# Weight conversions one step behind their raw loads, in program order on ScalarE, and handed out among more products, in a two-layer decoder step

## The chip, the cores and the metric

The kernel runs on one core of a Trainium2 chip. The metric is device time in microseconds (us) of one execution; the number given for a kernel is the median of several runs. The engines are TensorE (PE, matrix products), VectorE (DVE), ScalarE (ACT), GpSimd (POOL) and SyncE (SP), which here only issues transfers (DMAs). Each engine works through its own instructions strictly in the order in which they stand in its program; an instruction that waits holds up all behind it.

## The reference

One inference step of a two-layer decoder, for a prompt of 2048 positions and 8 sample streams of 4 positions. Layer 0 is a gated recurrent mixer (four heads), layer 1 is sliding-window attention over keys and values that are computed once. The change is in layer 0:

```python
def gla_mixer(h, state0, norm_g, w_in, w_gate2, b_gate, out_norm_g, w_out):
    u = rmsnorm(h, norm_g)
    proj = u @ w_in
    q, k, v, gate, g_low = jnp.split(proj, ...)
    log_a = jax.nn.log_sigmoid((g_low @ w_gate2 + b_gate)) / A_GATE_NORMALIZER
    o, state = gla_recurrence(heads(q) * dk ** -0.5, heads(k), heads(v), heads(log_a), state0)
    o = rmsnorm(o, out_norm_g).reshape(bsz, seq_len, BRANCH_WIDTH)
    return (o * jax.nn.silu(gate)) @ w_out, state
...
def step(state, blk):
    b = jnp.cumsum(ac, axis=2)
    scores = einsum('bhtd,bhsd,bhtsd->bhts', qc, kc, exp(b_t - b_s) where s <= t)
    out = einsum('bhtd,bhdv->bhtv', qc * exp(b), state) + einsum('bhts,bhsv->bhtv', scores, vc)
    new_state = exp(b_last) * state + einsum('bhsd,bhsv->bhdv', kc * exp(b_last - b), vc)
```

The model width is 1024, a head has 128 key and 512 value columns, and all inputs, weights and outputs are float32.

## The kernel before

**Products.** A float32 product is made of three fp16 matmuls: each operand is split into a high part (the fp16 rounding) and a low part (the rest), and high x high, high x low and low x high are added up in one PSUM bank. A weight therefore passes three steps before TensorE can use it: a DMA of 256 KB from DRAM into a float32 tile `wraw` (L224; three buffers), the high part on ScalarE (L192: scale by the norm's gain and round), and the low part on VectorE (L193: scaled weight less the high part). Both parts go into a tile `W` of a pool of `NW` buffers. `Unit.load` does all three for one half of a unit, and `Unit.steps` gives the two halves as two steps. `Cols` is a column group of a weight, made of units: a head's v weights and its g (gate) weights are four units each, eight steps; its q and k weights (`qk`) are units of 256-wide pieces.

**Order.** The program is written as lists of small steps that `run`, `weave` and `mix` play in turn; `weave(a, b)` spreads b among the steps of a. A scheduler then makes the order of each engine from the traced steps, by a model of time and by priorities. `tc.keep_in_program_order(x)` ties an instruction behind the one traced before it on its engine. It was used only for the weights that are converted ahead for layer 1 (`prepare`, tile `pst`, written back to DRAM as `pre`); these are done one step behind their raw load, by the list `pending` and `flush`.

**Layer 0.** It runs from about 100 to about 1130 us of the span, over four heads h and four blocks j of 512 positions, in the loop over n = 4h + j (block 14 is n = 14). Block n's own products are, for each of four groups c of 128 positions, v (`vg_steps(c, (0,))`) and gate (`vg_steps(c, (1,))`), 24 matmuls each (`pj`). Between them stand the q and k products of the next block (`qk_steps`, evicted by ACT at L457 into KQ), the decays of the next block (`decay_steps`: L379 to L385 with two table loads on ACT, E and bt), the recurrence of the block's chunks (`chunk_steps`: v is evicted at L192 and L193; `kv`, `o` and `lev` are its matmuls; S is the state, Sh and sth its fp16 halves, X and qe the decayed keys and queries), and the gate's eviction `sg` (L500) and the gated result `og` (L617). `og` is split into `ogT`, transposed by a DMA (L630, `ogk`), and written to DRAM (L631, `ogd`); that write stands on SP behind its transposition and waits for its end.

At the end of a head (j = 3, "last") the weights of the next head come in: all eight v steps run in one piece after the v products, ahead of the last three gate products, and all eight g steps in one piece behind the last gate product. The q and k weights come in one block earlier, at c = 0 of j = 2. The block behind that, j = 0 of the next head ("late"), makes its gate product for c = 0 after the next block's q and k products. In the last head the out-projection's weights come instead: `wo` and `wo1` are its two halves, with tiles in `uT` buffers and `W` buffers; 4 steps of `wo` and 8 of `wo1` run in block 14, `wo.steps()[4:]` (12 steps) in place of the next head's v, `wo1.steps()[8:]` in place of g.

Of the kernel before, what the change touches and what calls it, by code (L numbers as in the profile page):

```python
# [10 lines left out]
F16 = mybir.dt.float16  # L11
# [8 lines left out]
P = 128  # L20
# [5 lines left out]
AH, DK, DV = 4, 128, 512  # L26
# [24 lines left out]
NW = 12  # L51
# [24 lines left out]
def _body(tc, nc, cp, sb, ps, dr, i, o):  # L76
# [6 lines left out]
    def T(tag, shape, dt, bufs=None):  # L83
        return sb.tile(shape, dt, tag=tag, name=nm(tag), **({} if bufs is None else {"bufs": bufs}))
# [61 lines left out]
    def weave(main, fill):  # L146

        main, fill = list(main), list(fill)
        done = 0
        for n, f in enumerate(main):  # L150
            f()
            upto = len(fill) * (n + 1) // len(main)
            for g in fill[done:upto]:
                g()
            done = upto
        for g in fill[done:]:
            g()

    def run(steps):
        for f in steps:  # L160
            f()

    def mix(a, b):

        out = []
        weave([lambda f=f: out.append(f) for f in a], [lambda f=f: out.append(f) for f in b])
        return out

    def behind(steps, n):


        def one(f):
            with tc.high_priority(offset=-n):
                f()

        return [lambda f=f: one(f) for f in steps]
# [15 lines left out]
            put(act(hi, src, AF.Copy, scale=sc))  # L192
            dve.scalar_tensor_tensor(lo, src, sc, hi, ALU.mult, ALU.subtract)  # L193

    pending = []

    def flush():
        while pending:
            pending.pop(0)()

    class Unit:

# [5 lines left out]
        def steps(self):  # L208
            if self.pre is not None:
                return [self.fetch]  # L210
            return [lambda half=half: self.load(half) for half in range(2)]

        def raw(self, half):

# [25 lines left out]
                split((dst(0)[:, d], dst(1)[:, d]), raw[:, d], gs[:, k : k + 1], put=put)  # L240

        def load(self, half):
            if self.t is None:
                self.t = T("W", [P, 2, 1024], F16, NW)
            self.convert(half, self.raw(half), lambda hl: self.t[:, hl, half * 512 : half * 512 + 512])

        def prepare(self):

            uniq[0] += 1
            self.pre = dr.tile([P, 2, 1024], F16, tag=f"pre{uniq[0]}", name=f"pre{uniq[0]}")  # L250

            def one(half):
                raw = self.raw(half)
                flush()

                def rest():
                    t = T("pst", [P, 2, 512], F16, 2)
                    self.convert(half, raw, lambda hl: t[:, hl], tc.keep_in_program_order)
                    nc.gpsimd.dma_start(self.pre[:, :, half * 512 : half * 512 + 512], t)  # L259

                pending.append(rest)

            return behind([lambda half=half: one(half) for half in range(2)], 200)
# [10 lines left out]
    class Cols:  # L274
# [7 lines left out]
                self.units.append(Unit([(0, ncol, w[k0 * P : (k0 + self.per) * P, c0 : c0 + ncol])], ncol, gs, [(k0 + n) % ng for n in range(self.per)]))  # L282

        def steps(self):
            return [f for u in self.units for f in u.steps()]

        def prepare(self):
            return [f for u in self.units for f in u.prepare()]
# [564 lines left out]
    gw = [GroupW(g) for g in range(NKV)]  # L853
# [3 lines left out]
    def form_steps(m):  # L857

        b, f = {}, {}

        def load():
            two = T("KQ", [P, 2, 512], F32, 1)
            for n, (r, z) in enumerate(((0, 0), (0, 1), (1, 0), (1, 1))):
                t = T("wraw", [P, 512], F32, 3) if n < 2 else two[:, n - 2]
                k = UP[m] + 2 * r
                nc.sync.dma_start(t, i["b_w_out"][0][k * P : (k + 1) * P, z * 512 : z * 512 + 512])
                b[r, z] = t
            f[0], f[3], f[5] = b[0, 0], b[1, 0], b[1, 1]

        def put(n):  # L870
            def sub(x, y):
                t = T("sth", [P, 512], F32, 2)
                pool.tensor_tensor(t, x, y, ALU.subtract)
                f[n] = t

            if n == 2:
                sub(b[0, 1], b[0, 0])
            elif n == 1:
                sub(b[1, 1], f[2])
            elif n == 4:  # L880
                sub(b[1, 1], b[0, 1])
            elif n == 6:
                sub(b[1, 0], f[1])
            t = T(tags[0], [P, 2, 512], F16, 2)
            tags.append(tags.pop(0))
            split((t[:, 0], t[:, 1]), f[n], SWB)
            nc.gpsimd.dma_start(wfd[n][:, m], t)

        return behind([load] + [lambda n=n: put(n) for n in (0, 2, 1, 3, 6, 5, 4)], 200)

    prep = [f for w in gw for f in w.prepare()] + behind([flush], 200) + [f for m in range(8) for f in form_steps(m)]

    def some(n=2):
        out = prep[:n]
# [17 lines left out]
    prep = [lambda n=n, w=w, hf=hf: rope_table(n, w, hf) for n in range(2) for w in range(2) for hf in range(2)] + prep  # L912

    hw = {0: head_weights(0)}
    cur = Blk(0, 0, hw[0])
# [14 lines left out]
    f = T("pst", [P, 7, 64], F32, 2)  # L930
# [4 lines left out]
    wo, wo1 = (out_w(i["a_w_out"][0], half, gs_o) for half in range(2))  # L935
    box_o = {}

    def wo_aside():
# [3 lines left out]
        for u in range(4):  # L942
            wo1.units[u].t = t[:, u]

    blocks = [(h, j) for h in range(AH) for j in range(NBL)]
    weave([f for c in range(4) for f in cur.vg_steps(c, (0,))] + cur.vg_steps(0, (1,)), cur.level_steps() + cur.decay_steps())
    prev_tail = []
    samp = None
    sparts = []

    for n, (h, j) in enumerate(blocks):
        nxt = None
# [9 lines left out]
        last = j == NBL - 1  # L962
        late = j == 0 and h > 0
        if n > 0:
            weave(cur.vg_steps(0, (0,) if late else (0, 1)), prev_tail)
        if last:
            samp = SampleA(h, cur.w)
            for f in samp.proj_steps():
# [6 lines left out]
        if last:  # L975
            ch = [cur.chunk_steps(c) for c in range(3)]
            weave([f for c in range(1, 4) for f in cur.vg_steps(c, (0,))], ch[0] + lv[:3] + ch[1][:3] + lv[3:5] + ch[2][:3])
            run(hw[h + 1].v.steps() if h + 1 < AH else wo.steps()[4:])
            for c in range(1, 4):
                weave(cur.vg_steps(c, (1,)), (ch[c - 1][3:] if c > 1 else []) + lv[3 + c * 2 : 5 + c * 2])  # L980
            for f in ch[2][3:]:
                f()
            run(hw[h + 1].g.steps() if h + 1 < AH else wo1.steps()[8:])
        else:
            for c in range(3):
                if n == len(blocks) - 2:
                    if c == 0:
                        wo_aside()
                    more = (wo1.steps()[:8] + wo.steps()[:4])[c * 4 : c * 4 + 4]
                else:  # L990
                    more = side[c * 2 : c * 2 + 2] if n < 2 else some(PR[j])
                weave(cur.vg_steps(c + 1, (0, 1) if n else (1,)), mix(cur.chunk_steps(c) + lv[(0,3,6)[c]:(3,6,8)[c]], sparts[(0,3,7)[c]:(3,7,99)[c]]) + more)
                if j == NBL - 2 and h + 1 < AH and c == 0:
                    hw[h + 1] = head_weights(h + 1)
                    for u in hw[h + 1].qk:
                        for f in u.steps():
                            f()
            sparts = []
        if n == 0:
            gain(gs_o, i["a_out_norm"][0], later)  # L1000
# [55 lines left out]
        cur = nxt  # L1056
# [794 lines left out]
```

## Time and profile before

| what | value |
|---|---|
| median of 3 runs | 2803.41 us |
| the 3 runs | 2795.48, 2803.41, 2803.76 us |
| the profiled execution, its own time | 2805.45 us |
| its span | 2803.6 us |
| mean granted clock of TensorE | 0.989 |
| first 100 us of the span and some more | start-up, layer 0's first projections |
| about 100 to 1130 us | layer 0, 16 blocks |
| from about 1130 us | the out-projection, shared keys and values, layer 1 |

The page's engines: PE is the matrix product's engine, PEld its weight loads (beside PE), and DVE, ACT, POOL, SP as above. The DMA queue of SP is shown as SPq. A row of the timeline gives the start, the duration, the engine, the line, the operation, output<-input by the program's names, and in brackets the idle time of that engine just before it and what released it. Because each engine works in order, an ACT instruction that waits for a DMA also keeps the ones behind it; the release named in another engine's row is then that ACT instruction and not the DMA.

### The profile page before, as it was taken

How to read it: one execution, taken by the hardware profiler on the slowest of the kernel's cores; microseconds unless marked ns; L12 is line 12 of the kernel's file. 1: busy time of each engine (PE TensorE's matmuls, PEld its weight loads, DVE VectorE, ACT ScalarE, POOL GpSimd, SP SyncE). 2: the span in 40 equal slices, each digit the busy share in tenths (PEclk: the TensorE clock that was granted, in tenths of full speed). 3: DMA queues.
4: the chain of work that ended last, by engine and by line, in shares of the span. 5: the costliest groups of instructions: out<-in, count | busy, mean ns of one | idle time of the engine just before them, and what ended most of it. 6: DMA issues, size and time to landing. Idle time of an engine off the chain costs nothing.

```text
span 2803.6 us, 51849 instructions
## 1 busy us (share of the span) xinstructions
PE 2705.6 (97%) x19266; PEld 1386.7 (49%) x19266; DVE 1704.4 (61%) x3474; ACT 1392.0 (50%) x3245; POOL 1135.7 (41%) x1604
## 2 busy tenths in 40 slices
PE   6899999999999999999999999999999999989999
PEld 4444544544454444445444555555555555544444
DVE  5655665666666664446414666677777767777653
ACT  6554655565556554433313555566666666541110
POOL 2342234333333331126306676666566657530000
PEclk9999999999999999999999999999999999989999
DMA  8462444433434354789746777978978879896431
GB/s 213 93 148 53 110 111 125 110 106 105 137 102 127 107 166 123 231 258 291 235 164 154 130 154 153 228 136 154 202 128 159 187 152 191 166 216 199 145 104 58
DMA packets 814470, 429.53 MB, mean 153 GB/s; under 512 B 649600, under 2 KB 723144, under 8 KB 814184
## 3 DMA queue, kind: packets, MB, share of 16 engines
q1 hardware_dynamic: 801256, 390.49, 59.6%
q0 software_dynamic: 10880, 35.66, 3.6%
q8 instruction: 150, 2.46, 0.4%
q14 instruction: 104, 0.85, 0.1%
q10 hardware_dynamic: 2080, 0.07, 0.0%
HBM read 178.75 MB, written 107.54 MB: 102 GB/s over the span
## 4 chain that ended last, share of the span: by engine, by line
PE 62%; DMA 10%; ACT 10%; DVE 7%; issue 5%; POOL 5%; SPq 1%; ACTq 0%; POOLq 0%; DVEq 0%
PE pj L102 37%; PE o L102 11%; PE tr L102 9%; PE kv L102 3%; ACT o L1286 2%; PE lev L102 2%; DVE v L193 2%; DMA pre<-pst 1%; DMA wraw<-in_a_w_in_dram 1%; ACT v L192 1%; DMA pst<-v 1%; POOL ogT L190 1%; DVE o L1281 1%; DMA W<-in_state_gla_dram 1%; DMA uT<-ogT 1%
## 5 line engine op out<-in xcount | busy, mean ns | idle before, releaser
L102 PE MATMUL pj<-W,uT 128*128 128x512 f16 x5088 | 1200.6, 381 | 5.9 <-ACT KQ L457 2.4
L102 PEld LDWEIGHTS <-uT 128*128 128x128 f16 x6976 | 651.4, 98 | 701.8 <-issue 28.5
L102 PE MATMUL tr<-W,uT 128*128 128x512 f16 x1536 | 365.5, 379 | 0.0
L102 PEld LDWEIGHTS <-X 128*128 128x128 f16 x2744 | 185.0, 98 | 140.8 <-issue 8.7
L1286 ACT ACTIVATE o<-o,mx 128x256 f32<-128x256 f32 (+1 forms) x384 | 168.6, 439 | 166.4 <-DVE mx L1281 162.5
L181 POOL TENSOR_SCALAR rs_m<-ss 128x1 f32<-128x1 f32 (+3 forms) x190 | 44.1, 232 | 502.6 <-DVE ss L1183 187.8
L102 PE MATMUL pj<-uT,W 128*128 128x512 f16 (+1 forms) x912 | 187.5, 355 | 27.9 <-DMA uT<-ogT 24.4
L1281 DVE CUSTOM_DVE_ANT_0 o<-o,madd,nsink 128x256 f32<-128x256 f32 (+1 forms) x384 | 183.9, 479 | 49.9 <-PE o L102 45.7
L182 POOL TENSOR_TENSOR rs_r<-rs_m,mhalf 128x1 f32<-128x1 f32 (+2 forms) x186 | 186.8, 1004 | 14.1
L193 DVE SCALAR_TENSOR_TENSOR v<-o,v 128x512 f16<-128x512 f32 (+1 forms) x192 | 128.8, 671 | 102.3 <-ACT v L192 100.1
L533 POOL TENSOR_TENSOR KQ<-KQ,bt 128x256 f32<-128x256 f32 x112 | 99.1, 884 | 223.5 <-DVE X L190 221.8
L102 PEld LDWEIGHTS <-W 128*128 128x128 f16 x2448 | 129.1, 98 | 114.7 <-issue 21.3
L102 PEld LDWEIGHTS <-v 128*128 128x128 f16 x976 | 95.1, 98 | 115.9 <-issue 2.4
L190 POOL TENSOR_TENSOR ogT<-og,ogT 128x512 f16<-128x512 f32 x68 | 84.1, 1237 | 128.2 <-ACT ogT L189 128.2
L189 ACT ACTIVATE X<-KQ 128x512 f16<-128x512 f32 x128 | 84.7, 662 | 83.5 <-PE lev L102 57.4
L102 PEld LDWEIGHTS <-sg 128*128 128x128 f16 x800 | 77.7, 98 | 93.4 <-issue 1.2
L102 PE MATMUL o<-gl,X 128*128 128x256 f16 (+1 forms) x768 | 114.5, 272 | 6.2 <-DMA X<-qe 5.9
L192 ACT ACTIVATE v<-o 128x512 f16<-128x512 f32 (+1 forms) x192 | 111.2, 579 | 3.5
L190 DVE TENSOR_TENSOR X<-KQ,X 128x512 f16<-128x512 f32 x128 | 98.2, 767 | 20.8 <-ACT X L189 19.1
L1286 ACT ACTIVATE lev<-lev,mx 128x256 f32<-128x256 f32 (+1 forms) x128 | 56.5, 441 | 104.8 <-DVE mx L1281 102.8
L396 POOL TENSOR_TENSOR bt<-bt 128x256 f32<-128x256 f32 (+6 forms) x112 | 47.1, 420 | 145.6 <-ACT bt L385 138.6
L259 POOL DMA_DIRECT2D pre<-pst x72 | 50.5, 704 | 134.2 <-DVE pst L193 103.0
(439 smaller groups left out, 4878.1 us busy)
## 6 DMA issues: line engine op xcount, KB each, us to landing
pre<-pst POOLq DMA_DIRECT2D x72, 256.0 KB, 4.0
W<-pre SPq DMA_DIRECT2D x36, 512.0 KB
ogd<-ogk SPq DMA_DIRECT2D x68, 256.0 KB
wraw<-in_a_w_in_dram SPq DMA_DIRECT2D x64, 256.0 KB
wraw<-in_b_w_in_dram SPq DMA_DIRECT2D x64, 256.0 KB
oge<-og SPq DMA_DIRECT2D x64, 256.0 KB
wraw<-in_a_w_out_dram SPq DMA_DIRECT2D x32, 256.0 KB
X<-in_x_prompt_dram SPq DMA_DIRECT2D x32, 256.0 KB
```

Of the source, the lines that this page charges most:

```text
L102: return order(nc.tensor.matmul(*a, **k))
L181: pool.tensor_scalar(m[:n, :k], ss, a, b, ALU.mult, ALU.add)
L182: pool.tensor_tensor(r[:n, :k], m[:n, :k], mhalf[:n, :k], ALU.pow)
L189: act(hi, src, AF.Copy)
L190: eng.tensor_tensor(lo, src, hi, ALU.subtract)
L192: put(act(hi, src, AF.Copy, scale=sc))
L193: dve.scalar_tensor_tensor(lo, src, sc, hi, ALU.mult, ALU.subtract)
L259: nc.gpsimd.dma_start(self.pre[:, :, half * 512 : half * 512 + 512], t)
L396: pool.tensor_tensor(dst, two[:, :, 0], two[:, :, 1], ALU.mult)
L533: pool.tensor_tensor(keys, keys, d[:, :, 1:2].to_broadcast([P, NB, m]), ALU.mult)
L1281: dve.tensor_tensor_reduce(pm[:, z], pm[:, z], madd.rearrange("p a b -> p (a b)")[:, (2 - nk) * P :], -0.125, nsink[:, g * GRP + h : g * G ...
L1286: act(pm[:, z], pm[:, z], AF.Exp, scale=-1.0, bias=nm_[:, h : h + 1], accum_out=bx["sum"][:, h : h + 1])
```

## The change

The conversion is no longer part of the step that starts the raw load. After the first head (`eager[0] = False`) `load` starts the raw DMA, then runs the conversion that the step before left in the list `coming`, and leaves its own there. So a conversion is traced one step later than its load; each list of steps from `Cols.steps` gets one step more that runs the last one (9 in place of 8; the 12 steps of `wo` become 13), and the q/k units are followed by a `flush(coming)`. The `W` tile of a unit is taken (`pair`) when it is first converted, not when it is first loaded. The high part's instruction on ACT is tied to its program order, as for `pst`. The first head's weights keep the old way.

The steps are also given out otherwise. The next head's v steps were run in one piece; now they are handed out over the gate products c = 1, 2, 3 of the head's last block (three steps each), and the next head's g steps, before in one piece at the end of that block, over `vg(0, (0,))` of the next block together with `prev_tail`, the rest of the last block's steps. The 13 steps of `wo` come as 5, 4 and 4; the last part of `wo1` is run as before.

```diff
-    pending = []
-    def flush():
-        while pending:
-            pending.pop(0)()
+    pending, coming, eager = [], [], [True]
+    def flush(todo):
+        while todo:
+            todo.pop(0)()
...
+        def pair(self):
+            if self.t is None:
+                self.t = T("W", [P, 2, 1024], F16, NW)
+            return self.t
...
         def load(self, half):
-            if self.t is None:
-                self.t = T("W", [P, 2, 1024], F16, NW)
-            self.convert(half, self.raw(half), lambda hl: self.t[:, hl, half * 512 : half * 512 + 512])
+            raw = self.raw(half)
+            if not eager[0]:
+                flush(coming)
+            put = (lambda x: x) if eager[0] else tc.keep_in_program_order
+            coming.append(lambda: self.convert(half, raw, lambda hl: self.pair()[:, hl, half * 512 : half * 512 + 512], put))
+            if eager[0]:
+                flush(coming)
...
         def steps(self):
-            return [f for u in self.units for f in u.steps()]
+            return [f for u in self.units for f in u.steps()] + [lambda: flush(coming)]
...
+    eager[0] = False
...
+    new = []
...
         if n > 0:
-            weave(cur.vg_steps(0, (0,) if late else (0, 1)), prev_tail)
+            weave(cur.vg_steps(0, (0,) if late else (0, 1)), mix(prev_tail, new))
+            new = []
...
-            run(hw[h + 1].v.steps() if h + 1 < AH else wo.steps()[4:])
+            new = hw[h + 1].v.steps() if h + 1 < AH else wo.steps()[4:]
             for c in range(1, 4):
-                weave(cur.vg_steps(c, (1,)), (ch[c - 1][3:] if c > 1 else []) + lv[3 + c * 2 : 5 + c * 2])
+                z = (len(new) + 3 - c) // (4 - c)
+                weave(cur.vg_steps(c, (1,)), mix((ch[c - 1][3:] if c > 1 else []) + lv[3 + c * 2 : 5 + c * 2], new[:z]))
+                del new[:z]
             for f in ch[2][3:]:
                 f()
-            run(hw[h + 1].g.steps() if h + 1 < AH else wo1.steps()[8:])
+            new = hw[h + 1].g.steps() if h + 1 < AH else []
+            if not new:
+                run(wo1.steps()[8:])
...
                     for u in hw[h + 1].qk:
                         for f in u.steps():
                             f()
+                    flush(coming)
```

What this makes of the engines' programs is shown at three places. In these rows stand the line, the operation, output<-input and the shape; the number behind a name counts the traced tiles, and lines of the changed kernel are 5 higher in `raw` and 9 higher behind `load` (L192 and L193 are the same).

First, ACT in block 14, from the split of the gated result (ogT) on. `uT<-wraw` is a conversion of an out-projection weight. Before:

```order
L192 ACTIVATE uT_11347<-wraw_11478,gso 128x512
L192 ACTIVATE uT_11347<-wraw_11486,gso 128x512
L192 ACTIVATE v_11217<-pj_11176 128x512
L192 ACTIVATE Sh_11271<-S_10757 128x512
L192 ACTIVATE uT_11347<-wraw_11494,gso 128x512
L500 ACTIVATE sg_11269<-pj_11228 128x512
L192 ACTIVATE uT_11347<-wraw_11500,gso 128x512
L379 ACTIVATE E_11295<-tr_11293,bgate 128x512
L380 ACTIVATE E_11295<-E_11295 128x512
L192 ACTIVATE uT_11347<-wraw_11636,gso 128x512
```

After:

```order
L192 ACTIVATE Sh_11271<-S_10757 128x512
L192 ACTIVATE v_11217<-pj_11176 128x512
L509 ACTIVATE sg_11269<-pj_11228 128x512
L388 ACTIVATE E_11295<-tr_11293,bgate 128x512
L389 ACTIVATE E_11295<-E_11295 128x512
L390 ACT_TABLE_LOAD
L390 ACTIVATE E_11295<-E_11295,half_b 128x512
L394 ACT_TABLE_LOAD
L394 ACTIVATE bt_11291<-E_11299 128x512
L466 ACTIVATE KQ_11318<-pj_11274 128x512
```

The conversions no longer stand ahead of v, the gate, the decays and KQ; the first of them now comes 9 rows behind this piece, after the X and the v of the next group.

Second, SP at the second boundary between heads (end of block 7). `wraw<-in_a_w_in` is a raw load, `ogk` a transposition, `ogd` the write that waits for it. Before:

```order
L630 DMA_TRANSPOSE ogk_6291<-ogT_6288 128x8x128
L631 DMA ogd_103<-ogk_6291 256x1x512
L224 DMA wraw_6503<-in_a_w_in_dram 128x512
L224 DMA wraw_6507<-in_a_w_in_dram 128x512
L224 DMA wraw_6692<-in_a_w_in_dram 128x512
L224 DMA wraw_6696<-in_a_w_in_dram 128x512
L224 DMA wraw_6701<-in_a_w_in_dram 128x512
L224 DMA wraw_6705<-in_a_w_in_dram 128x512
L224 DMA wraw_6710<-in_a_w_in_dram 128x512
L224 DMA wraw_6714<-in_a_w_in_dram 128x512
L630 DMA_TRANSPOSE ogk_6608<-ogT_6605 128x8x128
L631 DMA ogd_104<-ogk_6608 256x1x512
```

After (the last six of the eight v loads are among these rows):

```order
L640 DMA ogd_103<-ogk_6291 256x1x512
L229 DMA wraw_6547<-in_a_w_in_dram 128x512
L639 DMA_TRANSPOSE ogk_6584<-ogT_6581 128x8x128
L229 DMA wraw_6572<-in_a_w_in_dram 128x512
L640 DMA ogd_104<-ogk_6584 256x1x512
L229 DMA wraw_6591<-in_a_w_in_dram 128x512
L229 DMA wraw_6620<-in_a_w_in_dram 128x512
L639 DMA_TRANSPOSE ogk_6661<-ogT_6658 128x8x128
L229 DMA wraw_6646<-in_a_w_in_dram 128x512
L640 DMA ogd_105<-ogk_6661 256x1x512
L229 DMA wraw_6668<-in_a_w_in_dram 128x512
```

Before, the last two v loads and six of the eight g loads stood in one row ahead of the pair ogk_6608, ogd_104, and the last two g loads behind it. After, v2 to v7 stand between the pairs, and the last, wraw_6668, behind ogd_105; the g loads follow later, among the pairs of the next block.

Third, ACT just after that boundary (block 8), where KQ frees the PSUM bank for the product behind it. Before:

```order
L379 ACTIVATE E_6877<-tr_6875,bgate 128x512
L192 ACTIVATE v_6834<-pj_6727 128x512
L380 ACTIVATE E_6877<-E_6877 128x512
L381 ACT_TABLE_LOAD
L381 ACTIVATE E_6877<-E_6877,half_b 128x512
L795 ACTIVATE W_7062<-W_7062,sbt_6795 128x512
L192 ACTIVATE Sh_6788<-S_6299 128x512
L189 ACTIVATE qe_6853<-sqk_6155 128x32
L385 ACT_TABLE_LOAD
L385 ACTIVATE bt_6873<-E_6881 128x512
L457 ACTIVATE KQ_6900<-pj_6856 128x512
```

After, from the same E on:

```order
L388 ACTIVATE E_6877<-tr_6875,bgate 128x512
L192 ACTIVATE v_6840<-pj_6691 128x512
L192 ACTIVATE W_6720<-wraw_6709,gsa 128x512
L389 ACTIVATE E_6877<-E_6877 128x512
L192 ACTIVATE W_6720<-wraw_6718,gsa 128x512
L390 ACT_TABLE_LOAD
L390 ACTIVATE E_6877<-E_6877,half_b 128x512
L189 ACTIVATE ssm_6813<-k_1133_6810 128x96
L189 ACTIVATE qe_6851<-sqk_6155 128x32
L394 ACT_TABLE_LOAD
L394 ACTIVATE bt_6873<-E_6881 128x512
L192 ACTIVATE W_6756<-wraw_6735,gsa 128x512
```

The conversions of g0, g1 and g2 (`W<-wraw`) now stand in the chain from E to KQ (the row behind this piece is KQ, L466); before, all of g's conversions were done ahead of this place.

More of the change, by code (lines that the diff above doesn't have):

```diff
@@ L253, in one @@
                 raw = self.raw(half)
-                flush()
+                flush(pending)
                 def rest():
@@ L889, in form_steps @@
         return behind([load] + [lambda n=n: put(n) for n in (0, 2, 1, 3, 6, 5, 4)], 200)
-    prep = [f for w in gw for f in w.prepare()] + behind([flush], 200) + [f for m in range(8) for f in form_steps(m)]
+    prep = [f for w in gw for f in w.prepare()] + behind([lambda: flush(pending)], 200) + [f for m in range(8) for f in form_steps(m)]
     def some(n=2):
```

## The prediction

> **What bounds the kernel now.** I read the page's first part, then busy time by stretches of the span, and then the rows of the stretches where TensorE stands still.
>
> ```profile
> PE 2705.6 (97%) x19266; PEld 1386.7 (49%) x19266; DVE 1704.4 (61%) x3474; ACT 1392.0 (50%) x3245; POOL 1135.7 (41%) x1604
> ```
>
> TensorE (PE) is busy for 97% of the span and its 19,266 matmuls stay as they are, so the change can win only where PE idles and lose only where it makes PE idle. The recurrent layer runs from about 100 to 1130 us. By stretches (PE's busy time is the third number of a row, PEclk the granted clock):
>
> ```profile
> core 0: us, PE busy (x) PEld busy (x) DVE busy (x) ACT busy (x) POOL busy (x), PEclk, DMA share, GB/s
> 200.00:1000.00 800.00, 790.05 (x5294) 386.53 (x5292) 504.21 (x857) 446.96 (x792) 267.28 (x414) 1.00 0.41 110
> 1000.00:1050.00 50.00, 44.09 (x240) 20.04 (x238) 29.99 (x45) 29.10 (x47) 14.61 (x23) 1.00 0.58 162
> 1050.00:1200.00 150.00, 149.10 (x930) 71.77 (x928) 68.14 (x125) 64.29 (x123) 28.99 (x48) 1.00 0.62 182
> ```
>
> Idle time is 800 - 790.05 = 9.95, then 50 - 44.09 = 5.91, then 150 - 149.10 = 0.90: together 16.76 us, 0.6% of the span. That is the ceiling of any gain. The stretch 1000 to 1050, block 14, is by far the worst per microsecond. Its PE rows with an idle time in brackets, and ScalarE (ACT) beside them:
>
> ```profile
> 1011.89 0.38 PE L102 MATMUL kv<-v,ke 128*128 128x512 f16 x1 [1.79 <-ACT v L192]
> ...
> 1026.05 5.34 PE L102 MATMUL pj<-W,uT 128*128 128x512 f16 x24 [1.23 <-ACT KQ L457]
> ...
> 1032.53 1.46 PE L102 MATMUL pj<-W,uT 128*128 128x512 f16 x6 [1.14 <-ACT KQ L457]
> 1034.61 0.18 PE L102 MATMUL lev<-one_h,X 128*128 128x1 f16 x1 [0.62 <-ACT X L192]
> ...
> 1039.44 0.38 PE L102 MATMUL kv<-v,ke 128*128 128x512 f16 x1 [1.01 <-DVE v L193]
> ```
>
> ```profile
> 1010.63 0.72 ACT L192 ACTIVATE uT<-wraw,gso 128x512 f16<-128x512 f32 x1 [2.35 <-DMA wraw<-in_a_w_out_dram]
> 1011.26 0.58 ACT L192 ACTIVATE v<-pj 128x512 f16<-128x512 f32 x1
> ...
> 1029.11 0.72 ACT L192 ACTIVATE W<-wraw,gso 128x512 f16<-128x512 f32 x1 [2.21 <-DMA wraw<-in_a_w_out_dram]
> ```
>
> The page names v, KQ and X as the releasers, but the ACT rows show why these were late: ACT stood for 2.35 us at a conversion whose raw weight had not landed, and v, whose product was done, had to stand behind it.
>
> **The change part by part.** The number of instructions on every engine stays as it is; only their order moves, so no row is added and no row is removed.
>
> (a) Block 14. The conversions of the out-projection's weights leave the places ahead of v, KQ and X, as the ACT rows of the change show. The five gaps above go: 1.79 + 1.23 + 1.14 + 0.62 + 1.01 = 5.79. What is late next is ACT's own chain of decay and KQ; without the conversions it is ready before the product behind it ends, so I take all: **-5.8**, with 0 as the other end. The conversions come some 15 us later, in a row of products where PE waits for no one; their cover is the time until the second half of the out-projection reads the last of them:
>
> ```profile
> L192 ACT ACTIVATE W<-wraw,gso x24: 705/722/723, 1029.1 to 1132.1; 128x512 f16<-128x512 f32 x24
> ...
> 1139.22 5.34 PE L102 MATMUL o<-W,uT 128*128 128x512 f16 x24
> ```
>
> The last now starts at 1132.1 and is read near the end of the product that starts at 1139.22, about 1143.8: 11 us of cover, of which I expect 5 to 8 used. Nothing is charged; if the cover is gone, one load and conversion per late weight, about 4 us (worked out at e), is lost.
>
> (b) Start of block 15. One conversion waits 1.29 us for its load, and two small gaps follow:
>
> ```profile
> 1084.99 0.72 ACT L192 ACTIVATE W<-wraw,gso 128x512 f16<-128x512 f32 x1 [1.29 <-DMA wraw<-in_a_w_out_dram]
> ...
> 1086.22 0.18 PE L102 MATMUL lev<-sq,ssm 128*96 128x32 f16 x1 [0.50 <-ACT sq L189]
> 1086.69 5.57 PE L102 MATMUL pj<-W,uT 128*128 128x512 f16 x25 [0.30 <-DVE ssg L667]
> ```
>
> 0.50 + 0.30 goes: **-0.8**, at the other end 0.
>
> (c) q/k weights of the next head (block 2, first boundary). Four 256-wide conversions stand ahead of v and X:
>
> ```profile
> 212.86 1.69 ACT L192 ACTIVATE W<-wraw,gsa 128x256 f16<-128x256 f32 x4
> ...
> 215.65 0.51 PE L102 MATMUL lev<-X 128*128 128x64 f16 x12 [0.69 <-DVE S L545]
> ...
> 216.64 1.89 PE L102 MATMUL pj<-uT,W 128*128 128x512 f16 x8 [0.26 <-DVE v L193]
> ```
>
> 0.69 + 0.26 = 0.95 goes. In the new order all eight stand close together one block later, just ahead of an X; at 1.69 / 4 = 0.42 each that is 3.4 us of ACT, most of it beside a running product. I charge 0.5, one conversion more than PE's slack, with 0 and 3.4 as ends: **-0.45**.
>
> (d) First boundary between heads (about 345 us). PE has no gap here now:
>
> ```profile
> 334.20 0.52 SPq L631 DMA_DIRECT2D ogd<-ogk  x1
> ...
> 344.81 1.24 PE L102 MATMUL pj<-W,uT 128*128 128x512 f16 x5
> ```
>
> The last raw v load now follows the ogd at 334.20 directly, so its weight is converted some 4 us later (2.66 + 0.72 + 0.75, see e), near 340; the v product reads it at 344.81. Cover 4 us or so, **0**; without it, the sum of (e).
>
> (e) Second boundary. Here the change hands the eight v loads out over the last three gate products, and they come to stand on SP's queue among the transpositions ogk and the writes ogd. Rows of PE, SP and ACT there:
>
> ```profile
> 601.71 5.34 PE L102 MATMUL pj<-W,uT 128*128 128x512 f16 x24
> ...
> 612.98 0.38 PE L102 MATMUL kv<-v,ke 128*128 128x512 f16 x1 [0.41 <-ACT v L192]
> 613.64 0.27 PE L102 MATMUL lev<-sq,ssm 128*96 128x32 f16 x3 [0.28 <-DVE S L545]
> 614.29 4.91 PE L102 MATMUL pj<-uT,W 128*128 128x512 f16 x22 [0.39 <-DVE v L193]
> ...
> 620.18 2.10 PE L102 MATMUL pj<-W,uT 128*128 128x512 f16 x9
> ```
>
> ```profile
> 587.08 0.33 SPq L224 DMA_DIRECT2D wraw<-in_a_w_in_dram  x1
> ...
> 595.03 1.24 SPq L630 DMA_TRANSPOSE ogk<-ogT  x1
> 598.10 0.53 SPq L631 DMA_DIRECT2D ogd<-ogk  x1
> 598.74 1.59 SPq L224 DMA_DIRECT2D wraw<-in_a_w_in_dram  x2
> 600.67 1.26 SPq L630 DMA_TRANSPOSE ogk<-ogT  x1
> ```
>
> ```profile
> 589.74 0.72 ACT L192 ACTIVATE W<-wraw,gsa 128x512 f16<-128x512 f32 x1 [1.99 <-DMA wraw<-in_a_w_in_dram]
> ...
> L193 DVE SCALAR_TENSOR_TENSOR W<-wraw,gsa,W x96: 471/746/1646, 7.6 to 868.8; 128x512 f16<-128x512 f32 x64, 128x256 f16<-128x256 f32 x32
> ```
>
> Three prices come out of these. A write ogd starts 598.10 - 595.03 = 3.07 us after its transposition and keeps SP that long; a load behind the pair is issued 598.74 - 595.03 = 3.71 after the transposition. A load issued at 587.08 is converted from 589.74: 2.66. A conversion is 0.72 on ACT and, behind it, 0.75 on DVE (the middle one of the three numbers).
>
> The v product is 24 matmuls in 5.34 us, 0.216 from one start to the next. It reads the last weight, v7, at its 22nd matmul: 601.71 + 21 x 0.216 = 606.25. The v7 load now stands behind the pair that transposes at 600.67 at the latest; without the two loads ahead of it (1.59) that may be 599.08. So v7 is issued at 602.8 to 604.4, converted from 605.4 to 607.0, and its high half is there at 606.2 to 607.8. The stall is between 0 and 1.5; I take 1.15, nearer to the row as it stands.
>
> The g loads follow one block later than before. Three g conversions stand ahead of the KQ that frees the buffer for the g product (0.65 each from start to start; the state's W and Sh leave that place). KQ ends about when the g product can start, at 620.2, so nothing is charged. But with three raw buffers, g6's load waits for g3's conversion, which stands behind KQ: near 620.5, on DVE until 621.9; plus 2.66 and 0.72 gives g6 at 625.3, and g7, 0.65 to 0.75 behind it plus its wait for g4, at about 626 to 627. The g product reads g7 at 620.2 + 4.5 = 624.7. I charge **2.3** for the g weights, with 0 and a whole load and conversion, 4.1, as ends. The old gaps, 0.41 + 0.28 + 0.39 = 1.08, go. Sum: 1.15 + 2.3 - 1.08 = **+2.4**, ends -1.08 and 1.5 + 4.1 = +5.6.
>
> (f) Third boundary, the same walk against larger gaps of its own:
>
> ```profile
> 876.87 0.38 PE L102 MATMUL kv<-v,ke 128*128 128x512 f16 x1 [1.42 <-ACT v L192]
> 877.51 0.27 PE L102 MATMUL lev<-sq,ssm 128*96 128x32 f16 x3 [0.27 <-DVE S L545]
> 878.17 3.18 PE L102 MATMUL pj<-uT,W 128*128 128x512 f16 x14 [0.39 <-DVE v L193]
> ```
>
> 1.42 + 0.27 + 0.39 = 2.08 goes: 3.45 - 2.08 = **+1.4**, ends -2.08 and +5.6.
>
> Sum: -5.8 - 0.8 - 0.45 + 0 + 2.4 + 1.4 = **-3.25 us**. The profiled execution took 2805.45 us (span 2803.6 and 1.85 around it), so it would take 2802.2; it stands 2.04 above the median of the runs, 2803.41. On the median's basis the forecast is **2800.2 us**.
>
> A rule that speaks against this change, apart from the sum. The clock is at 1.00 in a stretch with 2.77 us of idle and at 0.83 in one with 4.18:
>
> ```profile
> 170.00:190.00 20.00, 15.82 (x81) 6.89 (x79) 14.57 (x21) 15.52 (x26) 17.08 (x24) 0.83 0.84 190
> 1030.00:1040.00 10.00, 7.23 (x40) 3.05 (x39) 9.17 (x13) 6.33 (x12) 3.51 (x4) 1.00 0.41 102
> ```
>
> The Trainium skill's page "TensorE: Matmul & The Clock Gate", Part 1 on the HAM clock gate, says that TensorE drops to half its clock after an idle window of about 3.4 us; both rows agree with it. By it my boundaries, with single stalls of at most 2.3, keep the full clock and the sum stands; a boundary that reached such an idle window would pay again at half clock.
>
> **The rivals.**
>
> *All touched gaps go and none comes* (faster). For it: an even hand-out leaves ACT 50% busy and DVE 61%, and (d) shows a boundary with slack. Against: SP's 3.07 us waits, and three raw buffers. Time: -5.79 - 0.80 - 0.95 - 1.08 - 2.08 = -10.7, 2792.7. Chance 0.20.
>
> *The raw loads queue behind ogk and ogd on SP* (slower). Each boundary waits for one more pair's 3.07 and one landing's 2.66, 5.73; three make 17.2, against 7.54 won at (a), (b) and (c): +9.6, 2813.0. It decides once v7's load falls behind one pair more than I count, that is, is issued after 604.4 at the second boundary. For it: the new order on SP; against: the first boundary has about 4 us of cover, and the third has 2.08 of gaps of its own that a later load takes up first. Chance 0.11.
>
> *The clock falls at the boundaries.* The row at 0.83 idles 4.18 and loses 0.17 x 20 = 3.4 by the clock, 7.6 in all; three boundaries make 22.7, less 7.0 won at (a) to (c): 2819.1. Against: nothing here idles that long. Chance 0.03.
>
> *Nothing moves that counts.* ACT is pinned to an order, and equal waits replace the old ones (each v or KQ then waits for a weight of its own): 2803.4. Chance 0.13.
>
> **How the numbers follow.** The forecast's own case, a net of a few microseconds, has 0.53. A measurement of this kernel can tell about 0.3% from no change, 8.4 us, that is below 2795.0 or above 2811.8. So faster 0.20, slower 0.11 + 0.03 = 0.14, same 0.53 + 0.13 = 0.66. The forecast with the ends of its terms reaches from -10.7 to about +8 (0 won at a to c, 5.6 lost at one boundary and 2.4 at another); the range goes from 2790.5, 2 us under the faster rival, to 2812.0, just short of the slower one. What it leaves out is the slower rival's upper part, the clock, and the ends of the rest, under 0.2.
>
> **What would show it.** (a): no ACT row waits for in_a_w_out raw weights between 1005 and 1035, and PE idles under 1.5 us in 1000 to 1050. (b), (c): no gap at about 1080 and 213. (e), (f): the v product of heads 2 and 3 broken once near its end, with W as the releaser (under 2 us), and the g product behind it broken near its end (about 2 us). PE's idle time from 200 to 1200 would be about 13.5 us. I would be wrong if the weights' conversions, pinned on ACT, keep v or KQ waiting elsewhere, or if the handed-out loads arrive so late that each boundary stands for more than 5 us.

## The result and the profile after

| | before | changed |
|---|---|---|
| median, 16 runs each | 2804.12 us | 2818.36 us |
| lowest to highest | 2795.48 to 2821.41 us | 2811.95 to 2827.45 us |
| profiled execution (span) | 2805.45 (2803.6) us | 2819.80 (2818.0) us |

The ratio is 1.005, with a 95% interval of 1.0039 to 1.0061: the changed kernel is slower by 14 us, where 2800.2 (2790.5 to 2812.0) had been predicted. PE of the changed kernel, from the first part of its page, and its busy time in the stretches of the prediction (same columns):

```profile
PE 2710.5 (96%) x19266; PEld 1386.1 (49%) x19266; DVE 1703.8 (60%) x3474; ACT 1390.3 (49%) x3245; POOL 1134.0 (40%) x1604
```

```profile
200.00:1000.00 800.00, 775.88 (x5170) 377.13 (x5169) 487.11 (x833) 436.23 (x773) 256.60 (x402) 1.00 0.40 106
1000.00:1050.00 50.00, 50.00 (x285) 23.60 (x284) 30.83 (x46) 26.01 (x44) 20.36 (x33) 1.00 0.50 133
1050.00:1200.00 150.00, 148.76 (x938) 71.94 (x936) 79.54 (x138) 71.14 (x136) 32.04 (x50) 1.00 0.67 190
```

The number of matmuls is the same, so the time has to lie in what PE waits for or in how long its matmuls take, the clock included. Block 14 has lost its idle time altogether, as predicted (5.91 before, 0 now). But from 200 to 1000 us PE now idles 24.12 us where it idled 9.95. To place this, the eviction of a gate (`sg`) serves as a milestone, since the gates follow one another in the same order in both kernels. Five of them, from ACT's timeline, first before, then changed:

```profile
283.12 0.60 ACT L500 ACTIVATE sg<-pj 128x512 f32<-128x512 f32 x1 [4.06 <-PE pj L102]
...
419.49 0.60 ACT L500 ACTIVATE sg<-pj 128x512 f32<-128x512 f32 x1 [1.61 <-PE pj L102]
...
682.33 0.58 ACT L500 ACTIVATE sg<-pj 128x512 f32<-128x512 f32 x1
...
947.91 0.58 ACT L500 ACTIVATE sg<-pj 128x512 f32<-128x512 f32 x1
...
1123.18 0.58 ACT L500 ACTIVATE sg<-pj 128x512 f32<-128x512 f32 x1
```

```profile
285.14 0.60 ACT L509 ACTIVATE sg<-pj 128x512 f32<-128x512 f32 x1 [4.06 <-PE pj L102]
...
429.85 0.60 ACT L509 ACTIVATE sg<-pj 128x512 f32<-128x512 f32 x1 [1.61 <-PE pj L102]
...
699.69 0.58 ACT L509 ACTIVATE sg<-pj 128x512 f32<-128x512 f32 x1
...
969.88 0.58 ACT L509 ACTIVATE sg<-pj 128x512 f32<-128x512 f32 x1
...
1137.71 0.59 ACT L509 ACTIVATE sg<-pj 128x512 f32<-128x512 f32 x1
```

The changed kernel is behind by 2.02, 10.36, 17.36, 21.97 and 14.53 us. So the first boundary between heads costs 8.3 us, the second 7.0 and the third 4.6, and blocks 14 and 15 give back 7.4. That is 12.5 of the 14.4 us between the two spans; 2.0 are there ahead of the first boundary, but kernels that leave the heads' weights alone (below) are also 1.1 to 1.8 us late there, so these 2.0 can't be put down to the change. At the end of the spans the difference is 14.4, about what it is at 1123 us (14.5). Of the 19.9 us of the three boundaries, 14.2 are idle time (24.12 less 9.95) and 1.7 a stretch at a lower clock (last section); the other 4 are in neither, and where they lie stays open.

PE at the first boundary, where the prediction expected nothing (changed kernel; in brackets the idle time just before):

```profile
359.19 0.21 PE L102 MATMUL lev<-ssm 128*96 128x16 f16 x1 [1.30 <-ACT ssm L189]
...
362.47 3.18 PE L102 MATMUL pj<-W,uT 128*128 128x512 f16 x14 [1.03 <-ACT KQ L466]
...
367.10 0.49 PE L102 MATMUL lev<-ssm 128*96 128x16 f16 x3 [1.22 <-DVE S L753]
...
381.10 0.27 PE L102 MATMUL o<-Sh,ke 96*128 96x32 f16 x4 [2.25 <-DVE ke L779]
```

The v product had no gap here: v7, the last of the eight v weights, came in time, as counted. The releasers are ssm, S and ke, the small operands of the sample streams' own recurrence, which runs once per head just behind the boundary, and KQ. ACT shows why ssm and KQ are late:

```profile
352.11 0.72 ACT L192 ACTIVATE W<-wraw,gsa 128x512 f16<-128x512 f32 x1 [1.88 <-DMA wraw<-in_a_w_in_dram]
352.74 0.58 ACT L192 ACTIVATE v<-pj 128x512 f16<-128x512 f32 x1
353.34 1.28 ACT L390 ACT_TABLE_LOAD   x1
354.63 0.32 ACT L390 ACTIVATE E<-E,half_b 128x32 f32<-128x32 f32 x1
354.86 1.32 ACT L192 ACTIVATE W<-wraw,gsa 128x512 f16<-128x512 f32 x2
356.20 1.28 ACT L394 ACT_TABLE_LOAD   x1
357.49 0.23 ACT L394 ACTIVATE sbt<-E 128x32 f32<-128x32 f32 x1
357.63 0.67 ACT L388 ACTIVATE E<-tr,bgate 128x512 f32<-128x512 f32 x1
```

ACT stands for 1.88 us at a g conversion whose raw weight has not landed. v, and then a whole chain of table loads for the samples' decays (E 128x32 to sbt), stand behind it, with two more conversions in between; the block's own decay chain, which ends in KQ, starts only at 357.63, and ssm follows at 358.87. Before, the chain started at 350.03:

```profile
350.03 0.67 ACT L379 ACTIVATE E<-tr,bgate 128x512 f32<-128x512 f32 x1
```

S and ke are DVE's work. S stands on DVE right behind a split of the samples' state that waited for ACT:

```profile
366.26 0.69 DVE L193 SCALAR_TENSOR_TENSOR pst<-W,pst 128x512 f16<-128x512 f32 x1 [1.67 <-ACT pst L192]
```

ke (380.36 on DVE) stands at the end of a row that begins with an X that waited 0.68 us for ACT; how much of its 2.25 us goes back to the g conversions is not shown row by row.

At the second boundary one g conversion alone holds ssm, and PE with it (ACT, then PE):

```profile
633.55 0.72 ACT L192 ACTIVATE W<-wraw,gsa 128x512 f16<-128x512 f32 x1 [2.14 <-DMA wraw<-in_a_w_in_dram]
634.17 0.27 ACT L189 ACTIVATE ssm<-k 128x96 f16<-128x96 f32 x1
```

```profile
634.49 0.21 PE L102 MATMUL lev<-ssm 128*96 128x16 f16 x1 [0.97 <-ACT ssm L189]
```

This is what block 14 looked like before, an urgent instruction behind a conversion that waits for a landing. At the third boundary the same pair stands at 903.84 (waiting 2.29 us) and 904.47, with 0.82 us of PE's time behind it.

### The profile page after: what moved, and what is told of

Read it like the earlier page. It is cut to its first block, busy times and chain, and to the rows that moved or that the text cites. A ratio compares the mean times of both kernels' runs of the same rounds, so it can differ in the third digit from the quotient of the medians.

```text
span 2818.0 us, 51852 instructions
## 1 busy us (share of the span) xinstructions
PE 2710.5 (96%) x19266; PEld 1386.1 (49%) x19266; DVE 1703.8 (60%) x3474; ACT 1390.3 (49%) x3245; POOL 1134.0 (40%) x1604
## 4 chain that ended last, share of the span: by engine, by line
PE 64%; ACT 10%; DMA 9%; DVE 7%; issue 5%; POOL 4%; SPq 1%; ACTq 0%; DVEq 0%; POOLq 0%
PE pj L102 38%; PE o L102 11%; PE tr L102 10%; PE kv L102 3%; ACT o L1303 2%; DMA wraw<-in_a_w_in_dram 2%; PE lev L102 2%; DVE v L193 1%; ACT v L192 1%; DMA pst<-v 1%; POOL ogT L190 1%; DMA W<-in_state_gla_dram 1%; DVE o L1298 1%; DMA uT<-ogT 1%; ACT W L192 1%
## 5 line engine op out<-in xcount | busy, mean ns | idle before, releaser
L102 PE MATMUL pj<-W,uT 128*128 128x512 f16 x5088 | 1203.4, 381 | 12.8 <-ACT sg L509 4.5
L193 DVE SCALAR_TENSOR_TENSOR v<-o,v 128x512 f16<-128x512 f32 (+1 forms) x192 | 128.8, 671 | 103.5 <-ACT v L192 101.0
L192 ACT ACTIVATE v<-o 128x512 f16<-128x512 f32 (+1 forms) x192 | 111.2, 579 | 3.7
L102 PE MATMUL pj<-W,v 128*128 128x512 f16 x448 | 103.7, 379 | 0.0
```

The source lines that it names most:

```text
L102: return order(nc.tensor.matmul(*a, **k))
```

## The experiments

Two theories were set against each other first. **Tie:** the tie to program order, with three raw buffers, keeps loads and conversions late. **Hand-out:** giving the steps out over more products puts the loads late, whatever the tie. All kernels below are edits of the changed kernel unless a line says otherwise; ratios are to the kernel before on the same chip.

**Which half loses?** Only the out-projection's weights changed; the heads' weights in the old way:

```diff
-    eager[0] = False
...
         last = j == NBL - 1
+        eager[0] = h < AH - 1
...
-            new = hw[h + 1].v.steps() if h + 1 < AH else wo.steps()[4:]
+            new = [] if h + 1 < AH else wo.steps()[4:]
+            run(hw[h + 1].v.steps() if h + 1 < AH else [])
...
-            new = hw[h + 1].g.steps() if h + 1 < AH else []
-            if not new:
-                run(wo1.steps()[8:])
+            run(hw[h + 1].g.steps() if h + 1 < AH else wo1.steps()[8:])
+            new = []
```

> The three boundaries between heads go back to the old way; only the out-projection's weights (blocks 14 and 15) are converted behind and handed out. If the boundaries alone carry the loss (theory: 9 + 7 + 5 = 21 us of delay there), their delay is under 1.5 us here, blocks 14 and 15 gain 5 to 8 us less a wait of about 1.2 us at the last weight of the out-projection, and the time is 2797 to 2800 us. Rival: the out-projection's weights are part of the loss (4 us of delay after block 15); then no less than 2804 us.

Measured: 2799.36 us, ratio 0.9977 (0.9965 to 0.9988), inside the 2797 to 2800 us of the theory. And the other half, the heads' weights changed and the out-projection's not (`eager[0] = n >= len(blocks) - 2` in the loop, `wo.steps()[4:]` run in one piece):

> The other half: the heads' weights as in the change, the out-projection's as before. Theory: the boundaries' delay of about 21 us stays and block 14 keeps its gaps of 5.9 us, so the time is 2822 to 2828 us, above the change. Rival, boundaries and out-projection share the loss: 2812 to 2818 us.

Measured: 2826.34 us, ratio 1.0076 (1.0057 to 1.0095). The halves are as the theory had them: the out-projection's part gains, the heads' part loses some 21 us, more than the whole change.

**Tie or hand-out?** First the tie and the conversion one step behind, with v and g in one piece again:

```diff
-            new = hw[h + 1].v.steps() if h + 1 < AH else wo.steps()[4:]
+            new = [] if h + 1 < AH else wo.steps()[4:]
+            run(hw[h + 1].v.steps() if h + 1 < AH else [])
...
-            new = hw[h + 1].g.steps() if h + 1 < AH else []
-            if not new:
-                run(wo1.steps()[8:])
+            run(hw[h + 1].g.steps() if h + 1 < AH else wo1.steps()[8:])
+            new = []
```

> The conversions stay one step behind and tied to program order on ScalarE, but v and g steps of the next head run in one piece again. Theory pin: the tie, with three raw buffers, keeps loads and conversions late, so the boundaries still cost 10 us or more together, state loads come late as in the change, and the time is 2808 to 2818 us. Rival, the handing out is the cause: the boundaries cost under 3 us together and the time is 2796 to 2800 us.

Then everything but the tie:

```diff
-            put = (lambda x: x) if eager[0] else tc.keep_in_program_order
+            put = lambda x: x
```

> Handed out and one step behind as in the change, but not tied to program order on ScalarE. Theory pin: the scheduler takes the steps early again, the boundaries cost under 2 us each, block 14 has its old gaps again (about 6 us idle from 1000 to 1050), and the time is 2801 to 2806 us. Rival, the handing out is the cause: the boundaries keep 20 us and the time is 2815 us or more.

Measured: 2818.10 us, ratio 1.0049 (1.0033 to 1.0065), and 2815.77 us, ratio 1.0034 (1.0021 to 1.0048). The first is as the tie's theory had it, at the upper end of its 2808 to 2818 us. Its path is another one, though: its two largest gaps are of kv, which waits for the transposition of ke by a DMA (3.07 us at 622 and 2.48 at 890), so the tie's loss is shown, but not that it always runs by way of ssm. The second is a miss for both: 2801 to 2806 us, or boundaries that keep 20 us, had been expected; the time fits the rival, but the boundaries cost 7.9 us by the milestones (table below). Each of the two loses by itself, and together (the change, 1.005) they lose no more than the first alone. The next two kernels take the second apart: the hand-out alone (the line `eager[0] = False` left out, so that each conversion follows its load at once), and the conversion one step behind alone (no tie, one piece).

> Only the handing out: conversion at once behind its load, no tie. Theory: the handing out is what puts v behind ScalarE's chain of table loads at the second and third boundary, so gaps of about 1.9 us before kv stand there and the time is 6 to 11 us above before, like the kernel without the tie. Rival, the conversion one step behind does that: no such gaps and the ratio to before is 0.999 to 1.001.

> Only the conversion one step behind: no tie, v and g in one piece. Theory: it changes nothing by itself, ratio 0.999 to 1.001, boundaries as before within 1 us, block 14 idle about 6 us. Rival, it costs what the kernel without the tie lost: 6 to 11 us above before.

Measured: the hand-out alone 2816.57 us, ratio 1.0037 (1.0023 to 1.0052); one step behind alone 2804.71 us, ratio 0.9997 (0.9985 to 1.0009). Converting one step behind does nothing by itself, and the hand-out alone loses 10 us. PE's busy time at the three boundaries (same columns as above, stretches of 90, 100 and 110 us), of before, the changed kernel, the tie in one piece and the hand-out alone, in this order:

```profile
330.00:420.00 90.00, 88.95 (x599) 43.57 (x598) 58.87 (x113) 53.09 (x98) 32.58 (x51) 1.00 0.48 126
590.00:690.00 100.00, 98.56 (x651) 47.85 (x648) 65.07 (x122) 61.00 (x111) 30.75 (x48) 1.00 0.45 127
850.00:960.00 110.00, 105.88 (x685) 51.16 (x684) 68.07 (x127) 63.94 (x115) 34.14 (x55) 1.00 0.44 118
```

```profile
330.00:420.00 90.00, 83.27 (x570) 40.15 (x568) 63.50 (x119) 58.08 (x105) 31.89 (x48) 0.98 0.54 147
590.00:690.00 100.00, 92.49 (x624) 44.25 (x623) 71.44 (x130) 61.98 (x112) 29.93 (x45) 1.00 0.51 136
850.00:960.00 110.00, 101.82 (x682) 48.81 (x680) 76.38 (x138) 64.15 (x117) 32.11 (x49) 1.00 0.44 123
```

```profile
330.00:420.00 90.00, 83.24 (x568) 40.42 (x566) 61.25 (x116) 54.94 (x102) 31.77 (x51) 1.00 0.51 137
590.00:690.00 100.00, 93.19 (x629) 45.02 (x628) 69.06 (x130) 60.68 (x112) 30.12 (x49) 0.98 0.50 139
850.00:960.00 110.00, 101.98 (x677) 49.08 (x676) 74.41 (x139) 64.33 (x118) 31.37 (x51) 0.98 0.45 126
```

```profile
330.00:420.00 90.00, 86.24 (x586) 42.08 (x585) 57.47 (x111) 51.22 (x96) 31.86 (x51) 0.98 0.45 117
590.00:690.00 100.00, 96.65 (x652) 47.49 (x651) 66.70 (x128) 58.24 (x108) 31.33 (x50) 1.00 0.49 132
850.00:960.00 110.00, 104.30 (x685) 50.43 (x683) 69.51 (x132) 60.98 (x111) 32.46 (x50) 0.97 0.45 124
```

Idle time over the three: 6.6 us before, 22.4 changed, 21.6 with the tie in one piece, 12.8 with the hand-out alone, 6.8 with the step behind alone. So of the hand-out's 10 us, 6.2 are idle time; about 5 more are lost by the clock in this trace (0.98 and 0.97 in two of its rows). How its idle time comes about without any late weight is seen on ACT at the second boundary of that kernel, with the matmul that waits for it:

```profile
617.91 0.67 ACT L388 ACTIVATE E<-tr,bgate 128x512 f32<-128x512 f32 x1
618.61 0.63 ACT L389 ACTIVATE E<-E 128x512 f32<-128x512 f32 x1
619.15 0.70 ACT L804 ACTIVATE W<-W,sbt 128x512 f32<-128x512 f32 x1
619.87 1.28 ACT L390 ACT_TABLE_LOAD   x1
621.17 0.72 ACT L390 ACTIVATE E<-E,half_b 128x512 f32<-128x512 f32 x1
621.79 0.61 ACT L189 ACTIVATE ogT<-og 128x512 f16<-128x512 f32 x1
622.31 0.58 ACT L192 ACTIVATE v<-pj 128x512 f16<-128x512 f32 x1
```

```profile
622.94 0.38 PE L102 MATMUL kv<-v,ke 128*128 128x512 f16 x1 [1.84 <-ACT v L192]
```

No conversion and no landing is in this piece. The third boundary has the same gap of 1.84 us (at 887.92). Before, v stood directly behind the first E; here the scheduler has put it behind the second E, the sample's state, a table load, the third E and a split. The steps that are mixed into `prev_tail` and the gate products change the order in which the rest is traced, and the scheduler orders the urgent v differently.

**Is it v's tie or g's?** The tie left off for v, q and k, kept for g and the out-projection:

```diff
-    pending, coming, eager = [], [], [True]
+    pending, coming, eager, tied = [], [], [True], [False]
...
-            put = (lambda x: x) if eager[0] else tc.keep_in_program_order
+            put = tc.keep_in_program_order if tied[0] and not eager[0] else (lambda x: x)
...
         if n > 0:
+            tied[0] = True
             weave(cur.vg_steps(0, (0,) if late else (0, 1)), mix(prev_tail, new))
+            tied[0] = h == AH - 1
```

> The change, but the next head's v conversions (and q, k) are not tied; g's and the out-projection's last ones are. Theory: lateness comes from both ties; v arrives early and the v product is not held up, but the g conversions still stand in ScalarE's chain from E to KQ and the state's loads still come late, so the boundaries keep 3 to 6 us each and the time lies between 2808 and 2820 us. Rival, v's tie alone makes everything late: the boundaries cost under 2.5 us each.

Measured: 2810.00 us, ratio 1.001 (0.9995 to 1.0025); idle at the boundaries 6.00, 5.25 and 4.87 us, that is 5.0, 3.8 and 0.8 above before. The expectation holds for the first two and misses the third. All conversions of the out-projection are still tied here, not only the last ones, so the gain of blocks 14 and 15 is in this time. The milestones separate the two places (us later than before, from one trace of each kernel; the boundaries from the gate at 283.12 to that at 947.91, blocks 14 and 15 from there to 1123.18):

| kernel | three boundaries | blocks 14, 15 |
|---|---|---|
| the change | 19.9 | -7.4 |
| heads' weights only | 20.9 | -1.4 |
| tie and step behind, one piece | 17.8 | -7.7 |
| v, q and k not tied | 11.5 | -7.5 |
| hand-out alone | 10.1 | -0.8 |
| hand-out and step behind, no tie | 7.9 | 1.1 |
| step behind alone | 3.5 | -1.7 |
| out-projection only, two traces | 3.2, -1.7 | -7.3, -6.5 |

So the ties of v, q and k make some 8 us of the loss (19.9 against 11.5). What g's tie adds to the hand-out is not settled by the time: 11.5 stands against 10.1 and 7.9 without it, and traces of one kernel differ by 5. The kind of gap does change with it: PE waits for ke at all three boundaries (0.72 to 2.63 us) in each of the four kernels that tie g's conversions, and in none of the others, before included; and the hand-out's wait of 1.84 us for v is gone.

**Where does the gain come from?** The kernel that changes the out-projection's weights alone, without the tie:

> As the kernel with only the out-projection's weights changed, but without the tie to program order. Theory: the gain in block 14 comes from the tie alone, so PE idles about 6 us again from 1000 to 1060 us and the time is that of before within 3 us, ratio 0.999 to 1.001. Rival, the conversion one step behind gains by itself: PE idles under 2 us there and the ratio is 0.9965 to 0.9985.

And with the tie, but the 13 steps in one piece:

> As the kernel with only the out-projection's weights changed (which took 2799.36 us, ratio 0.9977), but their 13 steps in the last block in one piece and not handed out. Theory: the tie alone gives the gain, block 14 idles under 1 us and the ratio to before is 0.9965 to 0.9990. Rival, the handing out is part of it: the ratio is 0.999 or more.

Measured: without the tie 2804.25 us, ratio 0.9998 (0.9984 to 1.0012); in one piece 2800.10 us, ratio 0.9985 (0.9976 to 0.9995). Blocks 14 and 15 up to 1060 us, with the tie and without:

```profile
1000.00:1060.00 60.00, 60.00 (x351) 28.49 (x350) 36.02 (x54) 32.03 (x54) 19.30 (x31) 1.00 0.47 130
```

```profile
1000.00:1060.00 60.00, 55.65 (x315) 25.63 (x313) 36.82 (x55) 33.17 (x56) 18.22 (x29) 1.00 0.49 140
```

The gain is the tie's: with it no idle time, without it 4.35 us. With the 13 steps in one piece these blocks lose their idle time too. So the same tie wins in block 14 and loses at the boundaries. Whether handing these steps out adds something is not settled, as the intervals of 0.9977 and 0.9985 overlap.

**A version that beats both.** The q and k weights behind and tied as well (`eager[0] = False` ahead of their loads, `True` behind their flush), v and g in the old way:

> As the kernel with only the out-projection's weights changed, and the next head's q and k weights are converted one step behind and tied too, v and g as before. Theory: the q and k loads also have time, so the gap of 0.69 us at about 215 us shrinks and nothing else is lost at the boundaries: ratio to before 0.996 to 0.998. Rival: as soon as any of a head's weights is tied, v and g come late at the boundaries (over 2 us each) and the ratio is 0.999 or more.

Measured: 2791.47 us, ratio 0.9952 (0.9939 to 0.9966), more than any row of its profile accounts for (which is of its slowest execution, 2798.79 us). Both kernels were therefore run once more, side by side:

> The kernel with only the out-projection's weights changed, once more, on one chip with the next: ratio to before 0.9965 to 0.9988 again. It sets what the q and k weights add.

> The kernel with the out-projection's and the q and k weights changed, once more, on the same chip. The profile shows a gain of at most 1 us over the other, so by it the ratio is within 0.0005 of that kernel's. Rival: it is 5 us or more faster again (0.9952 was measured), from a place that the profiles have not shown.

Measured: 2794.11 us, ratio 0.9966 (0.9954 to 0.9978), and 2795.88 us, ratio 0.9967 (0.9955 to 0.9979). On one chip the two are the same: q and k add nothing that can be measured, and 0.9952 is best taken as scatter between sets of runs, since the same kernel gave 0.9967 in the second set. Changing the out-projection's weights alone is faster than before by 6 to 10 us and faster than the full change by some 20.

A fourth raw buffer, which would tell how much of the tie's loss is the ring of three, was not tried; that part of the tie's theory stays open.

## Why the prediction was wrong

- **(a), (b): right.** -6.6 was predicted; PE's idle time at both places is gone, and the milestones give -7.4. The cover at the out-projection was overrated: of 11 us, all was used, and 0.83 + 0.41 us are lost at its last weight:

```profile
1158.61 0.38 PE L102 MATMUL o<-W,uT 128*128 128x512 f16 x1 [0.83 <-ACT W L192]
1159.39 0.59 PE L102 MATMUL o<-W,uT 128*128 128x512 f16 x2 [0.41 <-DVE W L193]
```

- **(c): no gain to be seen.** -0.45 was predicted and the gaps near 213 were to go; the changed kernel still has 0.54 us at 213.22, where the kernel with only the out-projection's weights changed, which keeps the old q and k, has 0.51 and 0.26. The runs with q and k show no gain either.
- **(d): the step that failed most.** "Cover 4 us or so, 0" looked at v7's arrival alone, and v7 did arrive in time. 8.3 us were lost all the same: at ssm, KQ, S and ke, of which ssm and KQ stand behind the g conversions on ACT, and in a stretch of lower clock behind the wait for ke.
- **(e), (f): +2.4 and +1.4 were predicted, 7.0 and 4.6 came.** The stalls of the v product (near 617 and 888) and the g product (near 637 and 639) are of the predicted kind:

```profile
639.39 3.40 PE L102 MATMUL pj<-W,uT 128*128 128x512 f16 x15 [0.91 <-ACT W L192]
...
887.85 0.38 PE L102 MATMUL pj<-W,uT 128*128 128x512 f16 x1 [2.03 <-ACT W L192]
```

Their sizes are not. For v, 1.15 was foreseen at each; it was 0.41 at the second boundary and 2.03 + 0.41 at the third. For g, 2.3 was foreseen; it was 0.41 + 0.91 at the second and 0.41 at the third. So these stalls came to 4.6 us together, against 6.9 foreseen, and the excess lies elsewhere. What was left out is the samples' recurrence: ssm passes through ACT just there, between table loads, and S and ke through DVE behind work that waits for ACT. "KQ ends about when the g product can start, so nothing is charged" was nearly right for KQ (0.26 us at each of the two), but it checked one consumer of ACT's chain where there are more. It was also left out that new steps among the old ones make the scheduler order the old ones anew. The hand-out alone shows what that can cost, about 10 us.
- **The signs and the rivals.** The prediction's own sign of being wrong, that each boundary stands for more than 5 us, came true at two of the three. The slower rival (2813.0, chance 0.11) had nearly the right size, 17.2 us at the boundaries against 19.9, but the wrong path: not SP's pairs in front of v, but ACT's row behind g's landings. The clock rival (2819.1, chance 0.03) came nearest to the time, by luck: it has 3.4 us of clock at each boundary, and the changed kernel lost 1.7 us at one of them.
- **The clock rule.** Both rows were said to agree with an idle window of 3.4 us. The row at 0.83 does not: its idle time is two gaps of 2.14 and 2.04 us, each shorter than that, and the clock was already down between them (0.59 from 177.5 to 180). So the full clock that the prediction kept for stalls of at most 2.3 us had no support there, and a stall of 2.25 us did cost clock (below).

In short: the mechanism of the gain was right, and its price was worked out from the instructions that were known to wait, not from all that stand behind a tied conversion, nor from the new order that the hand-out gives the rest.

## What to carry to other kernels

A tie to program order on an in-order engine moves a wait, it does not remove it: it pays where the tied work has slack and what stands behind it is urgent (blocks 14 and 15, 5 to 8 us), and loses where the tied work itself is due soon (heads' weights, some 18 us with the tie and the step behind alone); so apply it place by place. When a conversion is put into an engine's row, list everything that stands behind it there up to the next idle time, and price each consumer, the small side computations too. And where a scheduler makes the order, handing steps out among others also reorders the others; look at the whole order at the tight places, not only at the rows of the steps that were moved.

## What the runs showed of the hardware

A gap of about 2 us can be followed by a stretch at a lower clock. Behind the 2.25 us gap at 381 us in the changed kernel the granted clock was 0.66 over 5 us:

```profile
380.00:385.00 5.00, 3.90 (x22) 1.72 (x23) 4.80 (x10) 1.24 (x2) 0.78 (x2) 0.66 0.57 148
```

That is 0.34 x 5 = 1.7 us lost, nearly as much as the gap itself. The same 0.66 over 5 us stands behind gaps of 2.23 us (out-projection only, from 930) and 2.50 us (hand-out alone, from 405). Length does not decide it. In the kernel without the ties of v, q and k, a gap of 2.63 us at 647 was followed by full clock. The other way round, the step behind alone lost clock behind a gap of 1.43 us with two small ones (0.27 and 0.39) right after it, where the kernel before kept full clock behind the same three gaps (1.42, 0.27 and 0.39, in the prediction's rows for the third boundary):

```profile
878.25 0.38 PE L102 MATMUL kv<-v,ke 128*128 128x512 f16 x1 [1.43 <-ACT v L192]
```

```profile
880.00:885.00 5.00, 5.00 (x17) 1.94 (x16) 2.09 (x6) 4.56 (x9) 0.90 (x2) 0.66 0.43 105
```

In two traces of one kernel (out-projection only) the stretch from the gate at 682 to that at 948, with the third boundary, lost 3.0 us by the clock in one and none in the other, so a few us can come and go this way. The Trainium skill's page on the clock gate ("TensorE: Matmul & The Clock Gate", Part 1) gives an idle window of about 3.4 us with half clock behind it. The 1.7 us agree with one such window, since 3.4 us at half clock lose 1.7; but the gaps that brought it on here were shorter than a window.
